# A one-core encoder layer on Trainium2: sum transfers at two points of a quad instead of three, stores and tiles moved, another product order in w_down, and dummy matmuls at the start

## The chip, the cores and the metric

The kernel runs on one core of a Trainium2 chip. The metric is the device time of one execution in microseconds, the median of the runs shown. Of the core's engines, PE (TensorE) multiplies matrices, DVE (VectorE), ACT (ScalarE) and POOL (GpSimd) work elementwise, and SP (SyncE) issues transfers. Transfers are issued by the sequencers of SP, POOL and, rarely, ACT, each with a queue of its own.

## The reference, cut to what matters

```python
D_MODEL = 2048; SEQ = 512; D_FF = 5632          # one layer, batch 1, float32
mod = (silu(c) @ w_ada + b_ada)[:, None, :]
sh_m, sc_m, gt_m, sh_f, sc_f, gt_f = split(mod, 6)
h = x * (1 + sc_m) + sh_m
y = mixer_sublayer(h, ...)     # linear recurrence (8 heads) and sparse attention (16 heads),
                               # merged by sigmoid gates, projected by w_out
x = layer_norm(ALPHA * x + (1 + gt_m) * y, ln1_g, ln1_b)
h = x * (1 + sc_f) + sh_f
y = (silu(h @ w_gate) * (h @ w_up)) @ w_down
x = layer_norm(ALPHA * x + (1 + gt_f) * y, ln2_g, ln2_b)
```

The change touches the start (silu(c)), the attention loop, and above all the last three lines: the two products with w_gate and w_up, the product with w_down, and the last norm.

## The kernel before

Weights stay in float32 in DRAM. Each weight tile is fetched into a tile `raw` (128x1024, 512 KB), and split into two parts of fewer bits: ACT writes the high part `whi` (L272), DVE the rest `wlo` = raw − whi (L273). The left operand is split in the same way, and a product is three matmuls (high·high at L237, two mixed ones at L238 and L239). PE keeps its sums in PSUM.

The products with w_gate, w_up and w_down are done over 2x2 blocks of both operands with seven products of blocks instead of eight (`SEVEN`, L127: p1, q7, r6, p2, q5, q4, p3). Four of them need sums of weight blocks: S1 = 21+22, S2 = S1+11, S3 = 21+11 and S4 = S2+12, where 11 to 22 name the blocks.

**Gate and up.** A group, called a quad, is the seven products of one 2x2 quad of w_gate or w_up: `("gu", n)`, even n for gate, odd n for up; 44 of them, 40 (n from 4) in one loop of steps, each step one product of 24 matmuls. For these 40, a table (`fetch`, L1253) gives the step at which SP issues the fetches of the four blocks, counted back from the quad's first step: 11 at 7 steps, 21 at 6, 22 and 12 at 5 (L1268). DVE adds the sums S1 to S4 (L1271 to L1285) in `raw` tiles, of which there are five. For the w_down groups (`("dn", n, cc)`, 22 of them) and the first quads the sums are made ahead by transfers from DRAM to DRAM, 512 KB each, on the POOL queue (`add_up`, L993): a first one that copies a block, then ones that accumulate. There are 208 such jobs in one list. `more(n)` takes the next n from it: four per attention head, some in the projections after it, and the rest in the gate/up loop, one at each of q7, r6 and p2 of a quad, each behind a small POOL copy (`pace`, L1602) that waits for that product's result. A job list of `sum_jobs` is ordered by kind: all copies into S3, all into S1, then accumulates into S3 and S1, then copies into S2, and so on.

After an up quad, `give` (L1423) makes from the activations the left operands of w_down (DVE, tiles `r`) and stores them in seven transfers of 128 KB (names d_p, d_q, d_r) on SP's queue (L1436). All transfers of SP run through one sequencer in program order: an issue that waits for its data holds the ones behind it.

**Down.** The loop goes on with 154 units (product, n, cc) of 12 matmuls of 512 columns: products in the order of `SEVEN`, and for each the 11 pairs n and 2 column halves cc. Beside it, generators called side lanes are advanced after every half unit. `base_side` (L1504) has POOL load two rows of norm weights (`ln`, L1510) and scale them (L1511), load a stored tile `base` of the residual (L1515), and DVE (L1519) and POOL (L1522, L1523) norm it. `end_side` takes finished output tiles: `join` multiplies by the gate row `gtf` (L1531), adds base (L1532) and takes norm statistics (L1533); `norm` (L1535) applies the last layer norm, half of it on ACT and POOL, half on DVE (L1544, L1545), and stores. The last four units keep their split weights (`KEEP`, tiles `wkeep`): p3 for rows t+2, run piece by piece so that the end can follow each piece.

The row `gtf` (1 MB, L1065) is loaded on the POOL queue before the gate/up loop, in the one buffer with the tag "row" of the constant pool. At the start PE spreads the vector c over the partitions (L192), ACT takes its silu, and the first product waits for weights and h.

Of the kernel before, what the change touches and what calls it, by code (L numbers as in the profile page):

```python
# [31 lines left out]
P = 128  # L32
D = 2048
T = 512
# [90 lines left out]


SEVEN = ("p1", "q7", "r6", "p2", "q5", "q4", "p3")  # L127
NP2 = NF // 2


# [9 lines left out]
def layer_kernel(ctx, tc, ws, wa, wada, xt, x, cin, bada, lbl, ghg, gcq, gckv, ln1c, lnrow, ident, lvm, dist, out):  # L140
# [51 lines left out]
        mmul(spread[i], one_t[:1], cond[:1, i * T:(i + 1) * T], start=True, stop=True)  # L192
    for i in range(4):
        nc.scalar.activation(cond[:, i * T:(i + 1) * T], spread[i], AF.Silu)
    del spread


# [802 lines left out]
            add_up(*jobs.pop(0))  # L1000

    for h in range(SAH):
        more(4)
        at_query(h)
        if h >= 2:
            at_transpose(h - 2)
        if h == SAH - 1:
            del cqn_hi, cqn_lo
            ylo = [big(f"yalo{i}") for i in range(2)]
            for n in range(HGH):  # L1010
                yar.append(heap("yarel"))
# [231 lines left out]
    for n in range(NPRE, 2 * NP2):  # L1243
        steps += [Unit(("gu", n), i) for i in SEVEN]
    nsteps = len(steps)
    steps += [Unit(("dn", n, cc), i) for i in SEVEN for n in range(NP2 // 2) for cc in range(2)]
    raws = {}

    fetch, adds = {}, {}
    for n in range(NPRE, 2 * NP2):  # L1250
        s = NPRE * 7 + (n - NPRE) * 7
        for ahead, what in ((7, "11"), (6, "21"), (5, "22"), (5, "12")):
            fetch.setdefault(s - ahead, []).append((("gu", n), what))  # L1253
        for ahead, what in ((3, "S3"), (3, "S1"), (2, "S2"), (-2, "S4")):
            adds.setdefault(s - ahead, []).append((("gu", n), what))
# [123 lines left out]
    def gu_use(u):  # L1379
        n, i = u.group[1], u.i  # L1380
        p, up = n // 2, n % 2
        ps = acc[n, CHAIN[i]][:, :H]
        t = tmp.setdefault(n, {})
        if i == "p1":
            t["e"] = heap("e")
            nc.scalar.activation(t["e"][:, :H], ps, AF.Copy)  # L1386
        elif i == "q7":
            t["yv"] = heap("yv")
            nc.scalar.activation(t["yv"][:, :H], ps, AF.Copy)  # L1389
            acc_copy[:] = [t["yv"][:, :1]]  # L1390
        elif i == "r6":
            nc.scalar.activation(t["yv"][:, H:], ps, AF.Copy)
            acc_copy[:] = [t["yv"][:, H:H + 1]]
        elif i == "p2":
            e = t.pop("e")[:, :H]
            acc_copy[:] = [e[:, :1]]
            if up:
                nc.vector.tensor_add(e, e, ps)
                nc.vector.tensor_mul(act[p][:, :H], act[p][:, :H], e)
            else:  # L1400
                a = act[p] = heap("act")
                nc.vector.tensor_add(a[:, :H], e, ps)
                nc.scalar.activation(a[:, :H], a[:, :H], AF.Silu)
        elif i == "q5":
            vq = heap("vq")[:, :H]
            t["c"] = heap("c") if up else heap("act")
            nc.scalar.activation(vq, ps, AF.Copy)  # L1407
            nc.vector.tensor_sub(t["c"][:, H:], t["yv"][:, :H], vq)
        elif i == "q4":
            c = t.pop("c")  # L1410
            nc.vector.tensor_sub(c[:, :H], ps, t.pop("yv")[:, H:])
            if up:
                nc.vector.tensor_mul(act[p + NP2], act[p + NP2], c)
            else:
                act[p + NP2] = c
                nc.scalar.activation(c, c, AF.Silu)
        elif up:
            a, b = act.pop(p), act.pop(p + NP2)
            nc.vector.tensor_mul(a[:, H:], a[:, H:], ps)
            give(p, a, b)  # L1420
        else:
            nc.scalar.activation(act[p][:, H:], ps, AF.Silu)
        if i in DONE:  # L1423
            del acc[n, CHAIN[i]]

    def give(p, a, b):

        r, q = heap("r"), heap("r")
        sub = nc.vector.tensor_sub
        sub(r[:, :H], a[:, :H], a[:, H:])  # L1430
        sub(r[:, H:], a[:, H:], b[:, H:])
        sub(q[:, :H], r[:, H:], a[:, :H])
# [40 lines left out]
    def dn_use(u):  # L1473
# [5 lines left out]
        for t in range(2):  # L1479
# [4 lines left out]
            elif i == "q7":  # L1484
                nc.scalar.activation(part["Y"][:, j], ps, AF.Copy)
            elif i == "r6":
                nc.vector.tensor_sub(part["V"][:, j], part["Y"][:, j], ps)
            elif i == "p2":
                nc.vector.tensor_add(part["E"][:, j], part["E"][:, j], ps)
                ends.append((t, cc, part["E"][:, j]))  # L1490
            elif i == "q5":
                nc.vector.tensor_sub(part["Y"][:, j], part["Y"][:, j], ps)
                ends.append((t + 2, cc + 2, part["Y"][:, j]))
            elif i == "q4":
                nc.vector.tensor_add(part["V"][:, j], part["V"][:, j], ps)
                ends.append((t, cc + 2, part["V"][:, j]))
            if CHAIN[i] != "V":
                del acc[CHAIN[i], cc, t]
            del ps

# [25 lines left out]
    st2 = [cp.tile([P, 24], FT, name=f"sf{t}", tag=f"st{t}") for t in range(NT)]  # L1526
    rows2 = []

    def join(t, c, y, ps=None):

        nc.vector.tensor_mul(y, y if ps is None else ps, gtf[:, c * T:c * T + T])  # L1531
        nc.vector.tensor_add(y, y, base.pop((t, c)))  # L1532
        nc.vector.bn_stats(st2[t][:, c * 6:c * 6 + 6], y)  # L1533
        done[t, c] = y

    def norm(t, c, mv, on_pool):

        z, g, b = done.pop((t, c)), rows2[0][c], rows2[1][c]
        if on_pool:
# [2 lines left out]
            nc.gpsimd.tensor_add(z, z, b)  # L1542
        else:
            nc.vector.scalar_tensor_tensor(z, z, mv[:, 0:1], g, op0=OP.subtract, op1=OP.mult)  # L1544
            nc.vector.scalar_tensor_tensor(z, z, mv[:, 3:4], b, op0=OP.mult, op1=OP.add)  # L1545
        (nc.scalar if on_pool and t == NT - 1 else nc.sync).dma_start(out[t * P:t * P + P, c * T:c * T + T], z)

    def end_side():

# [6 lines left out]
        for n in range(12):  # L1556
            while not ends:
                yield
            join(*ends.pop(0))
            yield  # L1560
            yield
        for t in range(2):
            mv = ln_scale(st2[t], "mv2")
            for c in range(4):
                norm(t, c, mv, c % 2 == 0)
                yield
                yield
# [7 lines left out]
    for step in range(len(steps)):  # L1575
# [19 lines left out]
        if step == 3 * NPRE + 2:  # L1595
            for t in range(NT):
                side.drain(t)
            assert not hraw
            gtf = gate_row(1, "gtf")
        if u.group[0] == "gu" and u.group[1] >= NPRE and u.i in ("q7", "r6", "p2"):  # L1600

            nc.gpsimd.tensor_copy(pace, acc_copy[0])  # L1602
            more(1)
        if step == nsteps - 1:
# [6 lines left out]
            for i in "EYV":  # L1611
                part[i] = big(i, FT)
            side.add(0, base_side())
            side.add(1, end_side())
    res = big("res", FT)
    for t in range(2):
        for cc in range(2):
            for u in steps[len(steps) - KEEP:]:
                if u.group[2] == cc:
                    dn_mm(u, t)  # L1620
            join(t + 2, cc, res[:, 2 * cc + t], acc["V", cc, t])
        if t == 0:
            side.drain(0)
            side.drain(1)
        mv = ln_scale(st2[t + 2], "mv2")
        for c in (2, 3, 0, 1):
            norm(t + 2, c, mv, c < 2 if t == 0 else c == 0)


# [101 lines left out]
```

## Time and profile before

| | |
|---|---|
| median of 3 runs | 2841.31 us (2840.8 to 2846.91) |
| the profiled execution, own time | 2842.75 us |
| its span in the trace | 2841.0 us |
| PE busy | 2757.5 us, 97% |
| DVE, ACT, POOL busy | 72%, 41%, 22% |
| chain that ended last | PE 78%, DVE 8%, DMA 7% |
| start, until PE is steadily busy | 0 to 44 us |
| mixer, attention, projections | 44 to about 1450 us |
| gate/up loop, first to last copy of a quad's first product (L1386) | 1560.28 to 2371.37 us |
| down units | about 2387 to 2811 us |
| last units and end | to 2841.0 us |

Read the busy shares as averages: PE is busy nearly all the time, so what matters is where it waits, and whom it waits for. In rows of a timeline the bracket gives the idle time of that engine before the row, and what ended it. Rows with SPq are transfer issues on SP's sequencer; their second column is how long the issue took the sequencer.

### The profile page before, as it was taken

The page shows a single profiled execution, that of the slowest core. Times are in us where ns is not written, and L with a number is a line of the kernel's source. Part 1 is how long each engine was busy: PE and PEld are TensorE (multiplying, and loading weights), DVE is VectorE, ACT ScalarE, POOL GpSimd, SP SyncE. Part 2 cuts the span into 40 slices and gives each one's busy share as a digit, 9 for nine tenths or more (in the row PEclk, how much of TensorE's full clock was granted, in tenths as well). Part 3 has the DMA queues.
Part 4 walks back from the last instruction along what each step waited for, and adds up shares of the span by engine and source line. Part 5 has one row for each costly group of instructions (what it writes and reads, how often), then busy time and mean ns, then how long its engine had stood idle before and what let it go on. Part 6 is the DMA issues. An engine that isn't in the chain of part 4 may idle for free.

```text
span 2841.0 us, 41802 instructions
## 1 busy us (share of the span) xinstructions
PE 2757.5 (97%) x16034; PEld 2425.5 (85%) x16034; DVE 2042.3 (72%) x2878; ACT 1161.8 (41%) x1725; POOL 636.3 (22%) x807
## 2 busy tenths in 40 slices
PE   7999999999999999999999999999989999999996
PEld 5778888888888888888889999899989999887885
DVE  7877787778852777446667776777767777766777
ACT  4334434333222555222255443444434444554443
POOL 0011133342010764312110112111111001443003
PEclk9999999999999999999999999999999999999998
DMA  9866445556974875977945657666676346888764
GB/s 378 311 209 216 158 155 175 178 181 202 325 264 148 237 240 174 336 203 213 272 145 178 233 199 193 189 193 217 181 187 168 127 145 205 277 275 276 236 222 167
DMA packets 194058, 609.86 MB, mean 215 GB/s; under 512 B 23201, under 2 KB 43217, under 8 KB 190785
## 3 DMA queue, kind: packets, MB, share of 16 engines
q1 hardware_dynamic: 149186, 450.63, 46.2%
q0 software_dynamic: 44384, 156.24, 20.5%
q8 instruction: 126, 2.06, 0.3%
q14 instruction: 74, 0.61, 0.1%
q10 hardware_dynamic: 288, 0.31, 0.0%
HBM read 564.09 MB, written 149.70 MB: 251 GB/s over the span
## 4 chain that ended last, share of the span: by engine, by line
PE 78%; DVE 8%; DMA 7%; issue 3%; ACT 2%; POOL 1%; SPq 0%; DVEq 0%; ACTq 0%; POOLq 0%
PE gb L229 6%; PE y L229 6%; PE ga L229 6%; DMA raw<-in_ws 5%; PE V L237 4%; PE V L239 4%; PE V L238 4%; PE qb L229 3%; PE pb L229 3%; PE g L229 3%; PE v L229 3%; DVE wlo L273 3%; PE pa L229 3%; PE early L229 2%; PE s L229 2%
## 5 line engine op out<-in xcount | busy, mean ns | idle before, releaser
L273 DVE TENSOR_TENSOR wlo<-raw,whi 128x1024 fp32r<-128x1024 f32 x458 | 568.1, 1252 | 265.5 <-ACT whi L272 263.7
L272 ACT ACTIVATE whi<-raw 128x1024 fp32r<-128x1024 f32 x458 | 482.4, 1058 | 479.3 <-DVE raw L1275 93.6
L359 DVE TENSOR_TENSOR wlo<-raw,whi 128x1024 fp32r<-128x1024 f32 (+1 forms) x228 | 284.5, 1251 | 110.0 <-ACT whi L347 109.5
L347 ACT ACTIVATE whi<-raw 128x1024 fp32r<-128x1024 f32 (+1 forms) x228 | 233.7, 1038 | 206.9 <-DVE raw L1082 72.3
L237 PE MATMUL V<-mhi,whi 128*128 128x256 f32 x1056 | 301.8, 286 | 14.8 <-ACT vq L1407 14.8
L239 PE MATMUL V<-mhi,wlo 128*128 128x256 f32 x1056 | 300.8, 285 | 0.0
L238 PE MATMUL V<-mlo,whi 128*128 128x256 f32 x1056 | 300.7, 285 | 0.0
L237 PEld LDWEIGHTS V<-mhi,whi 128*128 128x128 f32 x1056 | 204.4, 194 | 16.3 <-ACT vq L1407 16.1
L1602 POOL COPY pace<-yv 128x1 f32<-128x1 f32 x80 | 55.9, 699 | 691.5 <-ACT yv L1389 627.8
L239 PE MATMUL Y<-R,wlo 128*128 128x256 f32 x704 | 198.5, 282 | 11.2 <-DVE wlo L273 11.2
L239 PEld LDWEIGHTS V<-mhi,wlo 128*128 128x128 f32 x1056 | 204.4, 194 | 0.0
L238 PEld LDWEIGHTS V<-mlo,whi 128*128 128x128 f32 x1056 | 204.3, 193 | 0.0
L237 PE MATMUL Y<-R,whi 128*128 128x256 f32 x704 | 198.3, 282 | 1.0 <-ACT whi L272 1.0
L238 PE MATMUL Y<-R,whi 128*128 128x256 f32 x704 | 197.8, 281 | 0.0
L239 PEld LDWEIGHTS Y<-R,wlo 128*128 128x128 f32 x704 | 135.0, 192 | 12.6 <-DVE wlo L273 12.6
L238 PE MATMUL dnV<-wlo,fhi 128*128 128x512 f32 x336 | 132.7, 395 | 8.4 <-DVE wlo L273 8.3
L237 PEld LDWEIGHTS Y<-R,whi 128*128 128x128 f32 x704 | 135.1, 192 | 1.2 <-ACT whi L272 1.2
L238 PEld LDWEIGHTS Y<-R,whi 128*128 128x128 f32 x704 | 135.3, 192 | 0.0
L239 PE MATMUL dnV<-whi,flo 128*128 128x512 f32 x336 | 132.7, 395 | 0.0
L237 PE MATMUL dnV<-whi,fhi 128*128 128x512 f32 x336 | 132.4, 394 | 0.0
L993 POOL DMA_DIRECT2D sum_dn<-in_ws x132 | 96.6, 846 | 38.7 <-DMA sum_dn<-in_ws 31.2
L237 PE MATMUL V<-R,whi 128*128 128x256 f32 x352 | 98.2, 279 | 4.4 <-ACT e L1386 4.4
(450 smaller groups left out, 7562.4 us busy)
## 6 DMA issues: line engine op xcount, KB each, us to landing
raw<-in_ws SPq DMA_DIRECT2D x454, 512.0 KB, 5.0
sum_dn<-in_ws POOLq DMA_DIRECT2D x132, 512.0 KB, 9.4
raw<-in_wada SPq DMA_DIRECT2D x128, 512.0 KB, 5.0
raw<-sum_dn SPq DMA_DIRECT2D x88, 512.0 KB, 4.4
rawb<-in_wada SPq DMA_DIRECT2D x22, 1024.0 KB, 12.0
sum_dn<-sum_dn POOLq DMA_DIRECT2D x44, 512.0 KB, 6.5
sum_gu<-in_ws POOLq DMA_DIRECT2D x24, 512.0 KB, 8.7
raws<-in_wada SPq DMA_DIRECT2D x40, 256.0 KB, 6.9
```

The source lines that it names most:

```text
L229: mmul(*a, **k)
L237: f(ps, ahi, bhi, start=first, stop=False, **k)
L238: f(ps, ahi, blo, start=False, stop=False, **k)
L239: f(ps, alo, bhi, start=False, stop=last, **k)
L272: nc.scalar.activation(hi, src, AF.Copy)
L273: engine.tensor_sub(lo, src, hi.bitcast(FT))
L347: nc.scalar.activation(hi, src, AF.Copy)
L359: nc.vector.tensor_sub(lo, src, hi.bitcast(FT))
L993: nc.gpsimd.dma_start(d_sum[g, dst], block(g, src), **({"accum_op": OP.add} if add else {}))
L1602: nc.gpsimd.tensor_copy(pace, acc_copy[0])
```

## The change

The sum transfers in the gate/up loop are issued at q7 and q5 of a quad, not at q7, r6 and p2; every second attention head takes five in place of four. The fetches of a quad move to 8, 8, 6 and 4 steps ahead. Block 12 and the sum S3 no longer take `raw` tiles: they share a tile `wrow` in the buffer with the tag "row", so that `gtf` is loaded after the loop instead of before it. The stores of `give` move from SP's to POOL's queue. The order of products in w_down is p1, q7, r6, q5, p3, p2, q4. Rows t+2 are then finished first, through a part "R", with joins and norms spread over more yields; norms beside the products run on DVE alone. Six units are kept for the end; their piece is q4's. After the silu of c, 28 matmuls of 128x128 are issued whose results nobody reads.

```diff
+DOWN_SEVEN = ("p1", "q7", "r6", "q5", "p3", "p2", "q4")
...
+    for n in range(28):
+        mmul(spread[n % 4][:, :P], one_t, one_t, start=True, stop=True)
     del spread
...
     for h in range(SAH):
-        more(4)
+        more(4 + h % 2)
...
-    steps += [Unit(("dn", n, cc), i) for i in SEVEN for n in range(NP2 // 2) for cc in range(2)]
+    steps += [Unit(("dn", n, cc), i) for i in DOWN_SEVEN for n in range(NP2 // 2) for cc in range(2)]
...
-        for ahead, what in ((7, "11"), (6, "21"), (5, "22"), (5, "12")):
+        for ahead, what in ((8, "11"), (8, "21"), (6, "22"), (4, "12")):
...
-            r = raws[group, what] = new_raw()
+            if what == "12":
+
+                row = cp.tile([P, D], FT, name="wrow", tag="row")
+                raws[group, "S3"], r = row[:, :1024], row[:, 1024:]
+            else:
+                r = new_raw()
+            raws[group, what] = r
...
-                r = raws[g, "S3"] = new_raw()
-                add(r, raws[g, "21"], raws[g, "11"])
+                add(raws[g, "S3"], raws[g, "21"], raws[g, "11"])
...
-            nc.sync.dma_start(d_r[i, p // 2][:, p % 2], v)
+            nc.gpsimd.dma_start(d_r[i, p // 2][:, p % 2], v)
...
+        for t in (2, 3):
             mv = ln_scale(st2[t], "mv2")
             for c in range(4):
-                norm(t, c, mv, c % 2 == 0)
+                for _ in norm(t, c, mv):
+                    yield
...
-    KEEP = 4
+    KEEP = 6
...
-            gtf = gate_row(1, "gtf")
-        if u.group[0] == "gu" and u.group[1] >= NPRE and u.i in ("q7", "r6", "p2"):
+        if u.group[0] == "gu" and u.group[1] >= NPRE and u.i in ("q7", "q5"):
...
+            gtf = gate_row(1, "gtf")
             side.add(0, base_side())
             side.add(1, end_side())
-    res = big("res", FT)
+    side.drain(0)
+    side.drain(1)
...
+            ps, y, v = acc.pop(("Y", cc, t)), heap("y"), part["V"][:, 2 * cc + t]
+            nc.vector.tensor_mul(y, ps, gtf[:, (cc + 2) * T:(cc + 3) * T])
+            nc.vector.tensor_add(y, y, v)
+            nc.vector.bn_stats(st2[t][:, (cc + 2) * 6:(cc + 3) * 6], y)
...
+        for c in (0, 1, 2, 3):
+            for _ in norm(t, c, mv, c == 0, nc.scalar if c == 0 else nc.sync):
+                pass
```

On SP's queue in the middle of the gate/up loop, the kernel before issues the seven stores of a pair of quads (d_p, d_q, d_r; act and r are the activations) between the fetches of two quads each:

```order
L1436 DMA d_p_6_10665<-act 128x256
L1436 DMA d_q_6_10676<-r 128x256
L1436 DMA d_r_6_10687<-r 128x256
L1436 DMA d_p_6_10698<-act 128x256
L1436 DMA d_q_6_10709<-r 128x256
L1436 DMA d_q_6_10720<-r 128x256
L1436 DMA d_p_6_10731<-act 128x256
L1268 DMA raw<-in_ws 128x1024 x8
L1436 DMA d_p_7_10666<-act 128x256
```

and the changed kernel, in the same stretch:

```order
L1278 DMA raw<-in_ws 128x1024 x3
L1278 DMA wrow<-in_ws 128x1024
L1278 DMA raw<-in_ws 128x1024 x3
L1278 DMA wrow<-in_ws 128x1024
L1278 DMA raw<-in_ws 128x1024 x3
```

The stores have left SP's queue, and the fourth fetch of each quad goes to wrow.

On POOL's queue where the gate/up loop ends and the down units begin, the kernel before has the last pace copies and then the rows of `base_side`:

```order
L1602 COPY pace<-yv 128x1 x2
L1602 COPY pace<-e 128x1
L1510 DMA ln_22638<-in_lnrow 128x512
L1511 TENSOR_SCALAR ln_22638<-ln_22638 128x512
L1510 DMA ln_22639<-in_lnrow 128x512
L1511 TENSOR_SCALAR ln_22639<-ln_22639 128x512
L1515 DMA base<-d_z 128x512
```

and the changed kernel:

```order
L997 DMA sum_dn_1_4_7313<-in_ws 128x1024
L1444 DMA d_p_10_10705<-act 128x256
L1444 DMA d_q_10_10716<-r 128x256
L1444 DMA d_r_10_10727<-r 128x256
L1444 DMA d_p_10_10738<-act 128x256
L1444 DMA d_q_10_10749<-r 128x256
L1444 DMA d_q_10_10760<-r 128x256
L1444 DMA d_p_10_10771<-act 128x256
L1069 DMA gtf<-d_row 128x2048
L1518 DMA ln_22587<-in_lnrow 128x512
L1519 TENSOR_SCALAR ln_22587<-ln_22587 128x512
L1518 DMA ln_22588<-in_lnrow 128x512
```

Seven stores, a last sum and the load of gtf now stand ahead of the first `ln`.

On DVE near the end of the down units, the kernel before does a join's three operations in a row between two splits of weights (V is an output part):

```order
L273 TENSOR_TENSOR wlo<-raw,whi 128x1024
L1531 TENSOR_TENSOR V<-V,gtf 128x512
L1532 TENSOR_TENSOR V<-V,base 128x512
L1533 BN_STATS sf_12018<-V 128x6
L1495 TENSOR_TENSOR V<-V,dnY 128x512 x2
L273 TENSOR_TENSOR wlo<-raw,whi 128x1024
L273 TENSOR_TENSOR flo<-raws,fhi 128x512
L1531 TENSOR_TENSOR V<-V,gtf 128x512
L1532 TENSOR_TENSOR V<-V,base 128x512
L1533 BN_STATS sf_12019<-V 128x6
```

and the changed kernel, where V only takes gtf and base there:

```order
L277 TENSOR_TENSOR wlo<-raw,whi 128x1024
L1577 TENSOR_TENSOR V<-V,gtf 128x512
L1579 TENSOR_TENSOR V<-V,base 128x512
L277 TENSOR_TENSOR wlo<-raw,whi 128x1024
L277 TENSOR_TENSOR flo<-raws,fhi 128x512
L1577 TENSOR_TENSOR V<-V,gtf 128x512
L1579 TENSOR_TENSOR V<-V,base 128x512
```

At most two operations of this side work now stand between two splits, and the two subtractions that read dnY have gone from this place.

## Rows read from the trace of the kernel before

**Rows 1.** Timeline of ACT, line L1386: start us, us, operation [idle before<-releaser].
```profile
1560.28 0.36 ACT L1386 ACTIVATE e<-V 128x256 f32<-128x256 f32 x1
1599.64 0.37 ACT L1386 ACTIVATE e<-V 128x256 f32<-128x256 f32 x1
...
1717.78 0.36 ACT L1386 ACTIVATE e<-V 128x256 f32<-128x256 f32 x1
...
1743.69 0.37 ACT L1386 ACTIVATE e<-V 128x256 f32<-128x256 f32 x1
...
2351.34 0.36 ACT L1386 ACTIVATE e<-V 128x256 f32<-128x256 f32 x1
```

**Rows 2.** Timeline of SP's issues, 1707 to 1726 us.
```profile
1707.65 0.33 SPq L1436 DMA_DIRECT2D d_p<-act  x1
1719.34 0.33 SPq L1436 DMA_DIRECT2D d_q<-r  x1
...
1722.59 2.92 SPq L1268 DMA_DIRECT2D raw<-in_ws  x4
```

**Rows 3.** Timeline of POOL, 1720 to 1727 us.
```profile
1725.41 1.10 POOL L993 DMA_DIRECT2D sum_dn<-in_ws  x1
```

**Rows 4.** Chain of waits, 1700 to 1780 us: start us, us, what.
```profile
1723.67 13.81 DMA raw<-in_ws
```

**Rows 5.** Transfers issued, 1560 to 1700, then 1710 to 1900: KB, median us to landing.
```profile
raw<-in_ws SPq DMA_DIRECT2D x29, 512.0 KB, 6.1
...
raw<-in_ws SPq DMA_DIRECT2D x32, 512.0 KB, 9.3
```

**Rows 6.** Timelines of SP and POOL, 2380 to 2400 us.
```profile
2388.86 0.33 SPq L1436 DMA_DIRECT2D d_q<-r  x1
...
2385.51 0.58 POOL L1510 DMA_DIRECT2D ln<-in_lnrow  x1 [4.38 <-DVE flo L273]
...
2398.93 0.59 POOL L1515 DMA_DIRECT2D base<-d_z  x1
```

**Rows 7.** Timelines of DVE and PE, 2404 to 2412 us.
```profile
2405.41 0.55 DVE L1519 TENSOR_SCALAR base<-base,mv 128x512 f32<-128x512 f32 x1 [4.79 <-DMA base<-d_z]
...
2411.07 0.51 PE L238 MATMUL dnV<-wlo,fhi 128*128 128x512 f32 x1 [0.90 <-DVE wlo L273]
```

**Rows 8.** Transfers issued, whole span, and line L993 in 1560 to 1700 (issue ns min/median/max).
```profile
gtf<-d_row POOLq DMA_DIRECT2D x1, 1024.0 KB, 7.3
...
L993 POOL DMA_DIRECT2D sum_dn<-sum_dn x21: 515/515/536, 1563.8 to 1686.0; - x21
```

**Rows 9.** Waits, 2391 to 2812 us: us in total, times, longest us.
```profile
PE dnV L238 <- DVE wlo L273: 8.3, 5, 3.2
```

**Rows 10.** Timeline of PE, 2779 to 2782 us.
```profile
2780.38 0.50 PE L238 MATMUL dnV<-wlo,fhi 128*128 128x512 f32 x1 [3.17 <-DVE wlo L273]
...
2781.30 0.63 PE L238 MATMUL dnV<-wlo,fhi 128*128 128x512 f32 x1
```

**Rows 11.** Timelines of DVE, 2817 to 2841 us, and of PE, 2821 to 2824 us.
```profile
2817.26 0.69 DVE L1531 TENSOR_TENSOR res<-dnV,gtf 128x512 f32<-128x512 f32 x1 [0.60 <-PE dnV L239]
...
2836.28 0.75 DVE L1545 SCALAR_TENSOR_TENSOR res<-res,mv,l 128x512 f32<-128x512 f32 x1
...
2822.32 0.40 PE L239 MATMUL dnV<-wkeep,flo 128*128 128x512 f32 x1
```

**Rows 12.** POOL's waits 915 to 1125 us, its timeline 965 to 975, chain 915 to 1000.
```profile
POOL sum_gu L993 <- DMA sum_gu<-in_ws: 9.2, 4, 3.0
...
969.47 0.73 POOL L1016 TENSOR_TENSOR first<-qb 128x256 f32<-128x256 f32 x1
...
978.00 3.56 PE s L229 x22
```

**Rows 13.** Timeline of PE, 0 to 24 us.
```profile
2.63 7.16 PE L192 MATMUL cond<-cond,one_t 1*128 1x512 f32 x8 [2.63 <-DMA cond<-in_cin]
...
21.49 0.79 PE L229 MATMUL a<-hTlo,whi 128*128 128x512 f32 x1 [2.24 <-DVE hTlo L467]
```

More of the change, by code (lines that the diff above doesn't have):

```diff
@@ L1392, in gu_use @@
             nc.scalar.activation(t["yv"][:, H:], ps, AF.Copy)
-            acc_copy[:] = [t["yv"][:, H:H + 1]]
         elif i == "p2":
             e = t.pop("e")[:, :H]
-            acc_copy[:] = [e[:, :1]]
             if up:
@@ L1407, in gu_use @@
             nc.scalar.activation(vq, ps, AF.Copy)
+            acc_copy[:] = [vq[:, :1]]
             nc.vector.tensor_sub(t["c"][:, H:], t["yv"][:, :H], vq)
@@ L1487, in dn_use @@
                 nc.vector.tensor_sub(part["V"][:, j], part["Y"][:, j], ps)
-            elif i == "p2":
-                nc.vector.tensor_add(part["E"][:, j], part["E"][:, j], ps)
-                ends.append((t, cc, part["E"][:, j]))
             elif i == "q5":
@@ L1493, in dn_use @@
                 ends.append((t + 2, cc + 2, part["Y"][:, j]))
[L1494 to L1497, printed above, removed]
+            elif i == "p3":
+                nc.scalar.activation(part["R"][:, j], ps, AF.Copy)
+                ends.append((t + 2, cc, part["R"][:, j]))
+            else:
+                nc.vector.tensor_add(part["E"][:, j], part["E"][:, j], ps)
+                ends.append((t, cc, part["E"][:, j]))
+            if i in ("q7", "p3", "p2"):
                 del acc[CHAIN[i], cc, t]
@@ L1527, in layer_kernel, with join, norm @@
     rows2 = []
-    def join(t, c, y, ps=None):
-        nc.vector.tensor_mul(y, y if ps is None else ps, gtf[:, c * T:c * T + T])
+    def join(t, c, y):
+        nc.vector.tensor_mul(y, y, gtf[:, c * T:c * T + T])
+        yield
         nc.vector.tensor_add(y, y, base.pop((t, c)))
+        yield
         nc.vector.bn_stats(st2[t][:, c * 6:c * 6 + 6], y)
         done[t, c] = y
-    def norm(t, c, mv, on_pool):
+    def norm(t, c, mv, on_pool=False, q=None):
         z, g, b = done.pop((t, c)), rows2[0][c], rows2[1][c]
@@ L1544, in norm @@
             nc.vector.scalar_tensor_tensor(z, z, mv[:, 0:1], g, op0=OP.subtract, op1=OP.mult)
+            yield
             nc.vector.scalar_tensor_tensor(z, z, mv[:, 3:4], b, op0=OP.mult, op1=OP.add)
-        (nc.scalar if on_pool and t == NT - 1 else nc.sync).dma_start(out[t * P:t * P + P, c * T:c * T + T], z)
+        (q or nc.sync).dma_start(out[t * P:t * P + P, c * T:c * T + T], z)
     def end_side():
@@ L1555, in end_side @@
                 nc.gpsimd.dma_start(rows2[n][c], lnrow[2 + n][:, c * T:c * T + T].to_broadcast([P, T]))
-        for n in range(12):
+        for n in range(8):
             while not ends:
                 yield
-            join(*ends.pop(0))
-            yield
+            for _ in join(*ends.pop(0)):
+                yield
             yield
         for t in range(2):
+            for cc in range(2):
+                v = part["V"][:, 2 * cc + t]
+                nc.vector.tensor_mul(v, v, gtf[:, (cc + 2) * T:(cc + 3) * T])
+                yield
+                nc.vector.tensor_add(v, v, base.pop((t, cc + 2)))
+                yield
+        for t in (2, 3):
             mv = ln_scale(st2[t], "mv2")
             for c in range(4):
-                norm(t, c, mv, c % 2 == 0)
+                for _ in norm(t, c, mv):
+                    yield
                 yield
+        del part["Y"], part["R"]
+        for n in range(4):
+            while not ends:
                 yield
-    KEEP = 4
+            for _ in join(*ends.pop(0)):
+                yield
+            yield
+    KEEP = 6
     for u in steps[len(steps) - KEEP:]:
@@ L1610, in layer_kernel @@
             small = lambda name, dt=FT: yp.tile([P, T], dt, name=name, tag="y")
-            for i in "EYV":
+            for i in "EYVR":
                 part[i] = big(i, FT)
+            gtf = gate_row(1, "gtf")
             side.add(0, base_side())
             side.add(1, end_side())
-    res = big("res", FT)
+    side.drain(0)
+    side.drain(1)
+    assert not jobs and not ends
     for t in range(2):
@@ L1620, in layer_kernel @@
                     dn_mm(u, t)
[L1621 to L1627, printed above, removed]
+            ps, y, v = acc.pop(("Y", cc, t)), heap("y"), part["V"][:, 2 * cc + t]
+            nc.vector.tensor_mul(y, ps, gtf[:, (cc + 2) * T:(cc + 3) * T])
+            nc.vector.tensor_add(y, y, v)
+            nc.vector.bn_stats(st2[t][:, (cc + 2) * 6:(cc + 3) * 6], y)
+            done[t, cc + 2] = y
+        mv = ln_scale(st2[t], "mv2")
+        for c in (0, 1, 2, 3):
+            for _ in norm(t, c, mv, c == 0, nc.scalar if c == 0 else nc.sync):
+                pass
 def token_order():
```

## The prediction

> **What bounds the kernel now.** I read the page's busy shares first: PE 97%, so a gain must come out of PE's own waits, or out of the start and the end. Then the timeline of one ACT line that recurs once a quad, which shows where the gate/up loop runs late; there the timelines of SP and POOL and the chain of waits for the reason; then the waits in the down units; then the last DVE and PE rows.
>
> The copy of a quad's first product (L1386) is a clock for the loop [rows 1]. From 1560.28 to 1599.64 are two quads, 39.36 us, while nothing is late. From 1560.28 to 2351.34 are 38 quads, 791.06 us; at 39.36 a pair they would take 19 x 39.36 = 747.84. So 43.2 us are lost in this loop. A late quad is that from 1717.78 to 1743.69: 25.91 us, 6.2 more than 39.36 / 2. In the stretch 1560 to 1700 no time goes, and the sums there are copies; the time goes while accumulating sums run.
>
> Why it is late: SP starts the first store of a pair at 1707.65, and the next at 1719.34, since it waits for DVE's `r` [rows 2]. For 11.4 us it can issue no fetch. Once the stores are out, it issues four fetches back to back at 1722.59, 2.92 us of sequencer time. At the same moment POOL issues its sums, the last at 1725.41 [rows 3]. The raw tile that comes of it takes 13.81 us in the chain [rows 4], where the median landing is 6.1 us in the quiet stretch and 9.3 in the late one [rows 5]. DVE's sums of blocks, the split and PE wait for that tile.
>
> **The change part by part.** The sum is made against the profiled execution's 2842.75 us, 1.4 above the median of 2841.31; the same 1.4 is taken off at the end.
>
> *Gate/up loop.* The seven stores leave SP, so its 11.4 us hold is gone. Fetches 11, 21 and 22 are issued a step or two earlier, block 12 a step later. A step is 19.68 / 7 = 2.81 us. Block 22 now has about three steps, 8.4 us, to the sum that reads it, block 12 about four, 11.2 us. Both cover the quiet landing of 6.1, and block 12 also the 9.3 [rows 5]; beyond that PE has three steps of split weights ahead of it. Two sums a quad, at products two steps or more apart, in place of three, thin out the bursts; the 44 accumulates in the loop stay 44, over 22 quads in place of about 15. Ends: all 43.2 back, or nothing (if the accumulates themselves, not the bunching, slow the fetches). I take −41, near the full end, because quads lose no time at all in the quiet stretch with the same SP burst: it needs burst and accumulates together, and both are made smaller. The issue of seven stores on POOL costs it 7 x 0.52 = 3.6 us a pair by the row of its sum issues [rows 8], of 39.36, on an engine busy 22%.
>
> The Trainium skill, "SBUF — State Buffer", section "SBUF: two separate sides", says that descriptors for transfers from POOL's queue can't be written while DVE runs an operation in a mode that holds the port that the two share. If that held here, seven stores issued beside a busy DVE would be stretched, say to 1.2 us each as an estimate, and the next part would be 7 x 0.7 = 5 us dearer. The trace does not agree: 21 sum issues took 515 to 536 ns with DVE 72% busy [rows 8].
>
> *From the loop to the down units.* Here the move costs. Before, POOL issues the first `ln` load at 2385.51 and the first base load at 2398.93, 13.4 us later, after two loads and two scalings [rows 6]. DVE waits 4.79 us for that tile at 2405.41, and PE, which needs the splits behind it, waits 0.90 at 2411.07 [rows 7]: the cover is just used up. After, POOL's queue has six stores that wait for data from 2388.86 on [rows 6], and `gtf`, ahead of that `ln`. Six stores and gtf at 0.52 end at 2388.9 + 7 x 0.52 = 2392.5, so the chain starts 7.0 us later; `gtf`, 1 MB, took 7.3 to land [rows 8] and shares the queue with the `ln` tiles. The base operation stands at the same place in DVE's order, so that what comes later PE pays. The shift is 7.0 if the rest runs as before, 7.0 + 7.3 = 14.3 if the load waits for all of gtf. It is less if the two loads go faster than before, when stores and fetches ran beside them. I take 8.5, nearest to the 7.0, plus 1.7 for about eight matmuls at the low clock after a PE wait (0.63 us each against 0.40 [rows 10, 11]): +10. Ends: 0 and +18.
>
> *Down units.* Five PE waits for `wlo`, 8.3 us [rows 9]. One is the 0.90 above. The longest is 3.17 at 2780.38 [rows 10], where a join's three operations in a row stand ahead of the splits and norms run beside them; after it matmuls show 0.63, the 1.2 GHz level in place of 2.4, some 1.7 us more. With one or two operations between splits, and no operation on POOL beside DVE's, I take −4 of these 4.9. Ends: nothing, or all but the 0.90 with the clock, −9.
>
> *End.* From the second piece's join at 2817.26 to 2841.0 are 23.7 us. PE's last matmul ends at 2822.7, and 18.3 us follow it [rows 11]. After, one more norm pair on DVE (2 x 0.75) makes 25.3. But two pieces of 18 matmuls still stand behind that join (36 x 0.229 = 8.2 us) in place of two of 12 (5.5). So 25.3 − 8.2 = 17.1 follow PE's end: −1.2. Ends −3 and +3 (two more norms at 0.75 each, or two joins fewer in the way).
>
> *Attention.* Eight more transfers, four by head 7. POOL waits 9.2 us in four waits for earlier sums [rows 12]. The nearest reader is `first`, written at 969.47, and PE comes to its use at 978.00: 8.5 − 0.73 = 7.8 us of cover. Each transfer adds about 0.5 of issue and 2.3 of wait (9.2 / 4), 2.8; four are 11.2 by head 7, so at worst 3.4 are uncovered there, and twice that if it recurs: 0 to +6. POOL's bias work has gaps before it, so I take +1.
>
> *Start.* The spread of c took 7.16 us for eight passes of 512 columns [rows 13], 0.22 per 128. 28 matmuls in two passes are 56 x 0.22 = 12.5 us from about 10, to about 23. The second product waits till 21.49 anyway [rows 13], so the delay is at most 1.5; a clock that is up earlier can give some 2 back (12 matmuls x 0.2). Between them I take 0; ends −2 and +3.
>
> Sum: −41 + 10 − 4 − 1.2 + 1 + 0 = −35.2. 2842.75 − 35.2 = 2807.5, less 1.4 is 2806.
>
> **The rivals.**
> *No junction cost.* The loads at the junction run faster without stores beside them, or DVE gets a reserve from an unstalled loop. For: the two `ln` loads shared the engines with stores and fetches. Against: the wait of 0.90 is there already. With all 43.2 back: 2841.3 − 43.2 − 4 − 1.2 + 1 = 2794.
>
> *The burst moves to POOL.* The stores wait on POOL for `r` as they did on SP, with the sum of the next quad behind them, so that sums and stores come out together with the fetches of 11 and 21, and half of the gain stays away: −20.5 in place of −41: 2826.5. For: the 11.4 us hold is data, not SP. Against: the fetches are no longer in that queue.
>
> *The accumulates are the price.* The 13.81 us come from accumulating transfers sharing the DMA engines with fetches, whoever issues them and when; the same 44 then cost the same 43, and the junction comes on top: 2841.3 + 10 − 4 − 1.2 + 1 = 2847, slower. It decides as soon as the loop gives back less than 5.8 (10 − 4.2). For: only stretches with accumulates lose time. Against: the late quads all have the four fetches issued in one burst just after the hold [rows 2]. The Trainium skill, "DMA: Bandwidth & Descriptors", section "Issuing engines are not separate DMA queues", speaks for this rival: it says that issuing from another engine saves only sequencer time, since all transfers share the same engines. By it the move of the stores alone would give the loop nothing but SP's hold; the trace shows that this hold is 11.4 us of sequencer time before the burst [rows 2].
>
> *A wash.* The junction at its dear end and a third of the gain cancel to within 0.2%.
>
> **How the numbers follow.** The forecast's case 0.47 (2798 to 2815), no junction cost 0.20, half of the loop 0.18, accumulates 0.10, wash 0.05. 0.2% is 5.7 us, about what a measurement here can tell from no change. Faster 0.47 + 0.20 + 0.18 = 0.85, same 0.05, slower 0.10. The range reaches from the second case with 4 us for a better end or down part, 2790, to the third with 5.5 for a dearer junction, 2832. It leaves out 0.15.
>
> **What would show it.** Right: the copies of L1386's counterpart 39.4 us a pair throughout, so that 38 quads take about 750; no SP issue with a hold over a few us; raw landings near 6; PE waiting some 8 us near 2375, behind a DVE wait for base of over 10; no PE wait of 3 us late in the down units; about 17 us between PE's last matmul and the end. Wrong: quads of 25 us while accumulates run, raw tiles of over 12 us in the chain, or PE waits for `whi` or `wlo` in the attention heads.

## The result, and the profile after

The changed kernel takes 2803.07 us (median of 4 runs, 2800.0 to 2807.84) against 2844.11 for the kernel before (4 runs): 41.0 us less, ratio 0.9855 with a 95% interval of 0.983 to 0.9881. The forecast was 2806 and 35.3 less than the median then shown. The profiled execution has a span of 2798.0 us against 2841.0. These 43.0 us divide as follows:

| stretch | before | after | difference | forecast |
|---|---|---|---|---|
| start to the first copy in the loop (first product of quad n = 4) | 1560.28 | 1561.24 | +1.0 | +1 |
| 38 quads of the gate/up loop | 791.06 | 747.89 | −43.2 | −41 |
| from there to the first down matmul | 36.07 | 36.09 | 0.0 | 0 |
| down units, to PE's last matmul | 435.31 | 436.48 | +1.2 | +10 − 4 |
| after PE's last matmul | 18.28 | 16.30 | −2.0 | −1.2 |

The timeline of ACT's copy of each quad's first product, which answers to [rows 1] (L1395 is L1386 of before):

```profile
1561.24 0.36 ACT L1395 ACTIVATE e<-V 128x256 f32<-128x256 f32 x1
1600.60 0.36 ACT L1395 ACTIVATE e<-V 128x256 f32<-128x256 f32 x1
...
1718.74 0.36 ACT L1395 ACTIVATE e<-V 128x256 f32<-128x256 f32 x1
...
1738.77 0.37 ACT L1395 ACTIVATE e<-V 128x256 f32<-128x256 f32 x1
...
2309.13 0.36 ACT L1395 ACTIVATE e<-V 128x256 f32<-128x256 f32 x1
```

A pair takes 39.36 us as in the quiet stretch before, and so do all 19, within 0.06. The quad that took 25.9 us takes 20.0, the longer of the two alternating quads that make 39.36.

What the 43.2 us of the kernel before were made of, its waits of PE from 1560 to 2352 us show (us in total, times, longest):

```profile
PE V L237 <- ACT vq L1407: 14.8, 6, 6.6
PE Y L239 <- DVE wlo L273: 10.4, 6, 2.3
PE V L237 <- ACT e L1386: 4.4, 4, 1.4
```

These are 29.6 us; the changed loop has no such wait. The other 13.6 are matmuls that follow each other more slowly: the granted clock was 0.5 in five stretches of the loop before, 23.9 us in all, and 1.00 in the whole of the changed loop. So nearly a third of the gain is not waiting but the pace of matmuls around the waits.

SP's timeline in the stretch of [rows 2], then POOL's, shows where the wait for `r` went:

```profile
1705.36 0.33 SPq L1278 DMA_DIRECT2D wrow<-in_ws  x1
1705.79 18.02 SPq L1278 DMA_DIRECT2D raw<-in_ws  x3
```
```profile
1711.62 0.88 POOL L1444 DMA_DIRECT2D d_p<-act  x1
1720.57 0.57 POOL L1444 DMA_DIRECT2D d_q<-r  x1 [8.07 <-DVE r L1439]
...
1724.57 0.88 POOL L997 DMA_DIRECT2D sum_dn<-in_ws  x1
```

POOL now waits 8.07 us for DVE, and a sum comes out behind the stores, but no fetch stands there. SP's 18 us are three fetches, the last of which waits for a free tile until 1723.48. SP's waits for a free tile from 1600 to 2300 us are long, up to 15.4 us, and cost the loop nothing:

```profile
SPq L1278 <- DVE wlo L277: 508.2, 36, 15.4
```

The transfers of 1710 to 1900 us, answering to the second of [rows 5]:

```profile
raw<-in_ws SPq DMA_DIRECT2D x28, 512.0 KB, 7.1
...
wrow<-in_ws SPq DMA_DIRECT2D x9, 512.0 KB, 7.7
```

At the junction, POOL's timeline, then DVE's and PE's, answer to [rows 6, 7]:

```profile
2346.94 0.57 POOL L1444 DMA_DIRECT2D d_q<-r  x1 [4.78 <-DVE r L1439]
...
2350.69 0.54 POOL L1518 DMA_DIRECT2D ln<-in_lnrow  x1
2361.50 1.50 POOL L1519 TENSOR_SCALAR ln<-ln 128x512 f32<-128x512 f32 x1 [10.27 <-DMA ln<-in_lnrow]
...
2368.13 0.58 POOL L1523 DMA_DIRECT2D base<-d_z  x1
```
```profile
2371.11 0.55 DVE L1527 TENSOR_SCALAR base<-base,mv 128x512 f32<-128x512 f32 x1 [15.13 <-DMA base<-d_z]
```
```profile
2372.84 0.80 PE L242 MATMUL dnV<-wlo,fhi 128*128 128x512 f32 x1 [8.01 <-DVE wlo L277]
2373.43 0.63 PE L243 MATMUL dnV<-whi,flo 128*128 128x512 f32 x1
...
2376.37 0.40 PE L241 MATMUL dnV<-whi,fhi 128*128 128x512 f32 x1
```

POOL waits 10.27 us for the first `ln`, DVE 15.13 for the base tile, PE 8.01; eight matmuls follow at the lower clock level (granted 0.5 from 2369.5 to 2376.3), as forecast. PE's waits for splits from 2340 us on ([rows 9]):

```profile
PE dnV L242 <- DVE wlo L277: 10.4, 3, 8.0
```

Beside the 8.0 only two short ones are left; the 3.17 late in the down units [rows 10] is gone. The end, DVE then PE, answers to [rows 11]:

```profile
2773.49 0.69 DVE L1650 TENSOR_TENSOR y<-dnY,gtf 128x512 f32<-128x512 f32 x1 [1.97 <-PE dnY L243]
...
2793.67 0.75 DVE L1556 SCALAR_TENSOR_TENSOR y<-y,mv,l 128x512 f32<-128x512 f32 x1
```
```profile
2781.30 0.40 PE L243 MATMUL dnY<-wkeep,flo 128*128 128x512 f32 x1
```

### The profile page after: what moved, and what is told of

It is laid out like the page before. It is cut to its first block, busy times and chain, and to the rows that moved or that the text cites. A ratio compares the mean times of both kernels' runs of the same rounds, so it can differ in the third digit from the quotient of the medians.

```text
span 2798.0 us, 41846 instructions
## 1 busy us (share of the span) xinstructions
PE 2750.3 (98%) x16090; PEld 2421.6 (87%) x16090; DVE 2040.0 (73%) x2892; ACT 1158.3 (41%) x1724; POOL 675.6 (24%) x911
## 4 chain that ended last, share of the span: by engine, by line
PE 90%; DVE 4%; DMA 3%; issue 2%; ACT 1%; POOL 1%; SPq 0%; DVEq 0%; POOLq 0%; ACTq 0%
PE gb L233 6%; PE y L233 6%; PE ga L233 6%; PE V L243 6%; PE V L241 6%; PE V L242 6%; PE qb L233 3%; PE pb L233 3%; PE g L233 3%; PE v L233 3%; PE Y L241 3%; PE Y L243 3%; PE Y L242 3%; PE pa L233 3%; PE early L233 2%; PE dnV L242 2%
## 5 line engine op out<-in xcount | busy, mean ns | idle before, releaser
L277 DVE TENSOR_TENSOR wlo<-raw,whi 128x1024 fp32r<-128x1024 f32 x376 | 468.4, 1253 | 235.4 <-ACT whi L276 235.3
L276 ACT ACTIVATE whi<-raw 128x1024 fp32r<-128x1024 f32 x376 | 397.5, 1058 | 345.2 <-PE dnV L243 132.8
L242 PE MATMUL dnV<-wlo,fhi 128*128 128x512 f32 x352 | 139.1, 395 | 10.4 <-DVE wlo L277 10.4
L243 PE MATMUL dnV<-whi,flo 128*128 128x512 f32 x352 | 138.7, 394 | 0.0
L276 ACT ACTIVATE whi<-wrow 128x1024 fp32r<-128x1024 f32 x80 | 84.4, 1055 | 84.7 <-DVE wrow L1284 84.7
L233 PE MATMUL ga<-hThi,whi 128*128 128x512 f32 x256 | 102.0, 398 | 0.0
```

What stands on the lines that cost most here:

```text
L233: mmul(*a, **k)
L242: f(ps, ahi, blo, start=False, stop=False, **k)
L243: f(ps, alo, bhi, start=False, stop=last, **k)
L276: nc.scalar.activation(hi, src, AF.Copy)
L277: engine.tensor_sub(lo, src, hi.bitcast(FT))
```

## The experiments

The theory from the prediction: the loop is late where two things meet, SP's hold behind the stores with a burst of fetches after it, and accumulating sums. Its rivals: three sums a quad alone, the fetch table and the buffers alone, the accumulates alone. The measure is the time of 38 quads, from each run's own trace. It is far sharper than a run's total: ten of these runs give 747.9 to within 0.05.

| run | 38 quads | down units | after PE's end | time |
|---|---|---|---|---|
| before (profiled) | 791.1 | 435.3 | 18.3 | 2842.75 |
| changed (profiled) | 747.9 | 436.5 | 16.3 | 2800.09 |
| a_stores_sp | 747.9 | 436.2 | 16.7 | 2798.46 |
| a_three_sums | 747.9 | 437.8 | 16.3 | 2802.83 |
| a_old_fetch | 747.9 | 438.0 | 16.3 | 2803.3 |
| b_copies | 748.3 | 434.6 | 19.8 | 2801.17 |
| b_stores_pool | 748.2 | 444.4 | 17.9 | 2809.96 |
| b_two_sums | 760.0 | 441.4 | 18.3 | 2822.2 |
| b_new_fetch | 747.9 | 438.6 | 18.3 | 2801.37 |
| a_keep4 | 747.9 | 436.5 | 19.0 | 2804.08 |
| a_again | 747.9 | 440.5 | 16.3 | 2805.99 (median) |
| a_gtf_late | 747.9 | 435.4 | 16.3 | 2802.83 |
| a_sp_gtf_late | 747.9 | 430.9 | 16.7 | 2795.89 (median) |
| a_no_dummies | 747.9 | 439.1 | 16.3 | 2804.62 |

**One edit of the changed kernel undone.** a_stores_sp:

```diff
-            nc.gpsimd.dma_start(d_r[i, p // 2][:, p % 2], v)
+            nc.sync.dma_start(d_r[i, p // 2][:, p % 2], v)
```

> The changed kernel with the seven stores of a pair back on SP's queue. Measure: 38 quads of the gate/up loop by the copy of each quad's first product (before 791.1 us, changed 747.9). Theory of the prediction (SP held for 11 us by the stores, then fetches in a burst while accumulates run): most of the loss comes back, 770 to 791, with SP holds of about 11 us and quads of 23 to 26 us in the accumulating stretch alone. Rival 'sums': three sums a quad are the cause, so it stays at 748 to 755. Rival 'fetch table and buffers': earlier fetches and the tile outside the five raw buffers are the cause, so it stays at 748 to 755 too. The junction to the down units should lose less than the changed kernel's 8.0 us, as POOL no longer has stores ahead of the norm rows: 0 to 4.

747.9: the theory's number fell. SP's hold is there, as its timeline shows, and costs nothing:

```profile
1704.33 2.31 SPq L1278 DMA_DIRECT2D raw<-in_ws  x2
1707.10 0.33 SPq L1444 DMA_DIRECT2D d_p<-act  x1
1718.84 0.33 SPq L1444 DMA_DIRECT2D d_q<-r  x1
```

From 1707.10 to 1718.84 SP issues no fetch. But the two fetches just before the hold are blocks 11 and 21 of a quad to come: the new table puts them ahead of the stores in SP's order, where the old one had them behind. The junction's PE wait was 4.85, more than the 0 to 4 expected.

a_three_sums:

```diff
-        if u.group[0] == "gu" and u.group[1] >= NPRE and u.i in ("q7", "q5"):
+        if u.group[0] == "gu" and u.group[1] >= NPRE and u.i in ("q7", "r6", "p2"):
...
+            acc_copy[:] = [t["yv"][:, H:H + 1]]
...
+            acc_copy[:] = [e[:, :1]]
...
-            acc_copy[:] = [vq[:, :1]]
```

> The changed kernel with one sum transfer at each of q7, r6 and p2 of a quad, as before. 38 quads: theory of the prediction: stores no longer hold SP, so little comes back, 748 to 758. Rival 'sums': 775 to 791, with late quads while accumulates run, until the list is empty, some 15 quads of them. Rival 'fetch table and buffers': 748 to 752.

747.9: three sums a quad are not a sufficient cause.

a_old_fetch, which also gives block 12 and S3 raw tiles again:

```diff
-        for ahead, what in ((8, "11"), (8, "21"), (6, "22"), (4, "12")):
+        for ahead, what in ((7, "11"), (6, "21"), (5, "22"), (5, "12")):
```

> The changed kernel with the fetches at 7, 6, 5 and 5 steps ahead again and with block 12 and S3 in the five raw tiles; gtf is still loaded after the loop. 38 quads: theory of the prediction: 748 to 760, since stores and sums are eased. Rival 'sums': 748 to 752. Rival 'fetch table and buffers': 775 to 791, with long waits of SP for a raw tile.

747.9: nor are the fetch table and buffers. Each of the three edits can be missed as long as the other two stand.

**One thing taken from the kernel before.** b_copies:

```diff
-        nc.gpsimd.dma_start(d_sum[g, dst], block(g, src), **({"accum_op": OP.add} if add else {}))
+        nc.gpsimd.dma_start(d_sum[g, dst], block(g, src), **({"accum_op": OP.add} if add and g[0] == "gu" else {}))
```

> The kernel before, with every accumulating transfer for the w_down sums made a plain copy of the same 512 KB (the sums of w_down are then not formed; the work of all engines is otherwise the same). 38 quads: if accumulates are a necessary part, no quad is late and it takes 748 to 753. If the hold of SP alone does it, the loss stays at 780 to 791; the stretch 1560 to 1700, where copies run and nothing is late, speaks against that.

748.3: the accumulates are necessary. With the same bytes written, three transfers a quad, SP's hold and the old table, 0.4 of the 43 us is left. How an accumulate differs from a copy shows in POOL's queue from 1710 to 1850 us (packets, MB, share of the 16 DMA engines' time), in the kernel before, then in b_copies:

```profile
q0 software_dynamic: 2812, 10.21, 38.6%
q0 software_dynamic: 3051, 11.13, 22.4%
```

Per MB the packets of the accumulating transfers took 1.9 times as long, on the engines that the fetches use too. Their issue took longer too, 0.81 us in the median against 0.52; which of the two makes the fetches late is not shown.

b_stores_pool is the reverse of the first edit, on the kernel before:

```diff
-            nc.sync.dma_start(d_r[i, p // 2][:, p % 2], v)
+            nc.gpsimd.dma_start(d_r[i, p // 2][:, p % 2], v)
```

> The kernel before with only the seven stores of a pair moved to POOL's queue. 38 quads (before 791.1, changed 747.9). Theory of the prediction, that SP's hold and the fetch burst behind it make the loss: 748 to 755 by this edit alone. Rival 'any one relief is enough' (undoing each edit alone left the loop at 747.9): 748 to 755 for this and for each of the next two. Rival 'fetch table and buffers first': 775 to 791 here, since the fetches of blocks 22 and 12 still come at 5 steps and the raw tiles stay five.

748.2: moving the stores alone gives the whole loop back, as the theory said; "fetch table and buffers first" is out. The fetches of 1710 to 1900 us land in 5.2 us (median) in place of 9.3, although the same accumulates run. But its down units take 444.4, 9.1 more than before: PE waits 4.07 at the junction, where POOL's stores stand ahead of the norm rows (3.2 more), 2.1 more at other places, and 3.9 are slower matmuls.

b_two_sums:

```diff
-        if u.group[0] == "gu" and u.group[1] >= NPRE and u.i in ("q7", "r6", "p2"):
+        if u.group[0] == "gu" and u.group[1] >= NPRE and u.i in ("q7", "q5"):
...
-        more(4)
+        more(4 + h % 2)
```

> The kernel before with two sums a quad (at q7 and q5) and five transfers at every second attention head. 38 quads: theory of the prediction: the hold is there, bursts are thinner: 760 to 780. Rival 'any one relief is enough': 748 to 755. Rival 'fetch table and buffers first': 775 to 791.

760.0: 31 of 43 us come back, at the theory's edge; "any one relief is enough" misses here. Its late quads are shorter, as ACT's copies in the stretch of the 25.9 us quad show:

```profile
1721.93 0.36 ACT L1386 ACTIVATE e<-V 128x256 f32<-128x256 f32 x1
1743.47 0.37 ACT L1386 ACTIVATE e<-V 128x256 f32<-128x256 f32 x1
```

21.5 us in place of 25.9.

b_new_fetch is the reverse of a_old_fetch on the kernel before, with the load of gtf after the loop:

```diff
-        for ahead, what in ((7, "11"), (6, "21"), (5, "22"), (5, "12")):
+        for ahead, what in ((8, "11"), (8, "21"), (6, "22"), (4, "12")):
...
+                row = cp.tile([P, D], FT, name="wrow", tag="row")
+                raws[group, "S3"], r = row[:, :1024], row[:, 1024:]
...
+            gtf = gate_row(1, "gtf")
             side.add(0, base_side())
```

> The kernel before with the new fetch table and the tile outside the raw buffers for block 12 and S3 (so gtf is loaded after the loop, ahead of the norm rows on POOL). SP still holds 11 us at the stores. 38 quads: theory of the prediction: some of the loss stays, 755 to 775. Rivals 'any one relief is enough' and 'fetch table and buffers first': 748 to 752. The junction should show the price of gtf alone: a PE wait of 4 to 6 us in place of 0.9, as the run with the stores on SP had 4.8.

747.9, where the theory wanted 755 to 775. Its transfers land no sooner than those of before in 1710 to 1900 us:

```profile
raw<-in_ws SPq DMA_DIRECT2D x28, 512.0 KB, 9.7
...
wrow<-in_ws SPq DMA_DIRECT2D x10, 512.0 KB, 8.2
```

So long landings as such are not the loss: with 9.7 us as with the 9.3 of before, PE never waits in this loop. Here too blocks 11 and 21 go out ahead of the hold. But the edit also gives the fetches a sixth tile (`wrow`), and no run has the new table with five tiles: which of the two does it is not shown. Of the three edits made alone, this is the only one that is within the range of the whole change (2801.37, one run). The price of gtf was overestimated: PE waits 2.15 at the junction, not 4 to 6.

**The end.** a_keep4:

```diff
-    KEEP = 6
+    KEEP = 4
```

> The changed kernel with four units kept for the end in place of six. By the prediction's working, two pieces of 12 matmuls (5.5 us) stand behind the second join in place of two of 18 (8.2), so 2.7 us more follow PE's last matmul: 19.0 in place of 16.3. Rival: DVE is not what orders the end and it stays at 16.3 within 0.5.

19.0, exactly the working's number: DVE's chain from the second join orders the end, and what counts is how much of PE's work still stands behind that join.

**The junction.** a_again is the changed kernel, timed again beside the next.

> The changed kernel again, timed on the same chip as the next. Expected some 41 us under the kernel before (ratio 0.9855), with the loop at 747.9 and the PE wait of 8.0 at the junction to the down units.

Median 2805.99 (ratio 0.9863, 0.9844 to 0.9882), 36.7 under the kernel before where some 41 were expected; the loop takes 747.9, the PE wait is 8.47.

a_sp_gtf_late, with the edit of a_stores_sp and:

```diff
-            gtf = gate_row(1, "gtf")
             side.add(0, base_side())
...
+        if step == nsteps + 22:
+            gtf = gate_row(1, "gtf")
```

> The changed kernel with the stores on SP's queue and the load of gtf 22 units later, behind the first norm rows. Theory of the prediction on the junction (stores and gtf ahead of the norm rows on POOL's queue make the base tile late, and PE pays): the PE wait there falls from 8.0 to about 1, the low clock behind it goes, and the down units take 428 to 431 in place of 436.5, so 6 to 8 us under the changed kernel, ratio 0.982 to 0.984 to the kernel before. Rival 'given back later': base tiles run at a fixed pace, so what is not waited for here is waited for at a later base tile: the down units stay at 434 to 437.

Median 2795.89 (2794.61 to 2798.67; ratio 0.983, 0.9811 to 0.9848), 10.1 under the changed kernel on the same chip, whose runs span 2803.18 to 2806.54. The down units take 430.9, inside the 428 to 431; that is 5.6 and 9.6 under the two profiled executions of the changed kernel. PE's wait at the junction is 6.2 and 6.7 shorter, so of the 10.1, more than the 6 to 8 expected, some 6 are the junction's; much of the rest is the slower pace of one execution described at the end. This is the fastest version. "Given back later" is out for it, but not in general: a_stores_sp waits 3.2 us less at the junction than the changed kernel, and its down units are only 0.3 shorter, with a new wait of 1.61 at 2425.0 and 1.4 more of slow matmuls. PE's wait at the first base tile:

```profile
2370.72 0.51 PE L242 MATMUL dnV<-wlo,fhi 128*128 128x512 f32 x1 [1.78 <-DVE wlo L277]
```

a_gtf_late has this diff alone, the stores still on POOL.

> The changed kernel with gtf 22 units later, its stores still on POOL. It parts the two pieces of the junction: gtf alone (stores on SP, gtf ahead) left a PE wait of 4.8 and both 8.0. If the pieces add up, the stores alone leave 3 to 4; if the last one to land decides, 0.9 to 2.

Neither number: the wait is 5.73. With neither in the way 1.78, gtf alone 4.85, stores alone 5.73, both 8.01: 3.1 and 3.9 over 1.78, together 6.2. They add up nearly, above a floor that I had set at zero.

The floor is a third piece, the last sum, which two sums a quad put 4.45 us ahead of the first down matmul. All runs together show how the pieces act. The base operation on DVE is given in us after the first down matmul, and PE's wait is that for the split behind it:

| run | ahead of the norm rows on POOL | base operation | PE's wait |
|---|---|---|---|
| before | nothing | 18.00 | below 0.15 |
| a_sp_gtf_late | sum | 19.66 | 1.78 |
| b_new_fetch | gtf | 20.03 | 2.15 |
| b_two_sums | sum | 21.74 | 3.85 |
| b_stores_pool | stores | 21.95 | 4.07 |
| a_stores_sp | sum, gtf | 22.73 | 4.85 |
| a_gtf_late | sum, stores | 23.61 | 5.73 |
| a_three_sums | gtf, stores | 25.15 | 7.27 |
| changed | sum, stores, gtf | 25.89 | 8.01 |

In each row but the first the wait is the base operation's time less 17.88, to 0.01: what delays the base tile, PE pays in full. In the kernel before, the matmul behind it waits too little to be listed; the 0.90 of [rows 7] is at the next split:

```profile
2407.14 0.50 PE L238 MATMUL dnV<-wlo,fhi 128*128 128x512 f32 x1
```

Why the same sum leaves 1.78 in one run and 3.85 in another is open.

**The start.** a_no_dummies:

```diff
-    for n in range(28):
-        mmul(spread[n % 4][:, :P], one_t, one_t, start=True, stop=True)
```

> The changed kernel without the 28 dummy matmuls. Prediction's term: 0, between -2 and +3, so the copy of the fourth quad's first product (1561.24) moves by less than 3 us. In the first 45 us: with the dummies PE's first products run at the 2.4 GHz level from the start, without them at the 1.2 GHz level for some 8 us; rival 'the clock counts': 2 to 4 us later at 45 us without them; rival 'the weights' stream decides': within 0.5 at 45 us.

The first product runs 0.48 us after the dummies, 0.79 without (PE's timeline of the changed kernel, then of this one):

```profile
9.87 8.60 PE L198 MATMUL cond<-one_t 128*128 128x128 f32 x56
18.23 0.48 PE L233 MATMUL a<-hThi,whi 128*128 128x512 f32 x1
20.63 0.50 PE L233 MATMUL a<-hTlo,whi 128*128 128x512 f32 x1 [1.92 <-DVE hTlo L471]
...
21.27 0.63 PE L233 MATMUL a<-hThi,whi 128*128 128x512 f32 x1
```
```profile
19.54 0.79 PE L231 MATMUL a<-hThi,whi 128*128 128x512 f32 x1 [9.79 <-ACT hThi L466]
```

But 1.92 us of waiting later the changed kernel's matmuls are at 0.63 too (granted 0.5 from 21.1 to 24.5). The copy of n = 4 comes at 1563.42 without the dummies, 1561.24 and 1563.79 in two executions of the changed kernel. At 45 us nothing is gained that shows: the next stage (tile `early`) starts at 49.1 without the dummies, at 47.5 and 49.0 with them. So the dummies' worth is below the spread, and the two rivals are not told apart.

## Why the prediction was right

**The loop, −41, was −43.2.** That all of it can be had was right. Both halves of the cause are shown: without accumulates (b_copies) or without the hold (b_stores_pool) the loop is whole. What I had not seen is that a third condition must hold as well, the old fetch table with five tiles. With the new one the hold remains and nothing is late (a_stores_sp, b_new_fetch); whether the earlier fetches or the sixth tile does it is not shown. The change thus carries two remedies that suffice each by itself, and a third, the two sums, that gives 31. The late quad of the prediction was 5.9 us late, not 6.2, since the two quads of a pair differ. Two signs of being right did not come: SP still shows holds, up to 15.4 us, with no loss, and fetches land in 7.1 us, not near 6.

**From the loop to the down units, +10, was about +8.5.** The wait grew from 0.90 to 8.01, 7.1, and eight matmuls at the lower level cost some 1.7 (0.43 apart in place of 0.229, by the timeline above), 1.4 more than the slow ones behind the wait before. The shift was sized from issues and the landing of gtf at 8.5; the base operation came 7.9 later (25.89 in place of 18.00). That this is so near is partly luck: the base issue came 22.9 us after the first down matmul (2368.13 − 2345.22) in place of 11.5 (2398.93 − 2387.41), 11.4 later, but the base tile then landed in 3.0 us in place of 6.5. The last sum was not in the prediction's list of what stands ahead. a_sp_gtf_late shows the mechanism: without stores and gtf ahead, most of it goes.

**Down units, −4, was the term most mis-sized: about −7.3.** With +8.5 at the junction and +1.2 in all, the rest gave −7.3. Four waits of 7.4 us in all became two of 2.4: −5.0; matmuls further apart than 0.229 us, outside the junction, cost 3.6 before and 1.2 after: −2.4. The two late waits, 3.2 and 1.8 to 2.0 us, are in all five runs of the kernel before and its variants and in none of the changed kernel's. That the order of products, the spread joins or the norms on DVE alone removed them is argued from the order of DVE's operations: no run undoes one of these.

**The end, −1.2, was −2.0.** The chain from the second join took 24.5 us (2773.49 to 2798.0), not 25.3. The 8.2 us of PE behind it were right, and a_keep4 confirms the working.

**Start, 0, can't be told from the spread.** The 28 dummies took 8.60 us and ended at 18.47, not 12.5 and 23, so they did not delay the second product.

**Attention, +1, was 0.** The first uv matmul to the first pb matmul takes 219.8 us in both kernels (910.8 to 1130.6, 911.9 to 1131.7). POOL's wait for earlier sums did grow, from 9.2 [rows 12] to 12.9, under cover. The +1.0 at 1560 is there by 442 us, and is part of the spread: that copy lay between 1558.8 and 1565.4 over the runs.

**The rivals.** "No junction cost" is out (8.01). "The burst moves to POOL": the hold did move there, 8.07 us, and cost the loop nothing, since the fetches no longer stood behind it. "The accumulates are the price" is out: the same 44 run, and the loop is whole. They are a necessary condition, not a price. The Trainium skill says that another issuing engine saves only the sequencer's time to initiate a transfer ("DMA: Bandwidth & Descriptors", "Issuing engines are not separate DMA queues"). In these traces initiating is the small part, 0.33 us for a store on SP [rows 2]. What b_stores_pool took off SP was above all the wait for data, 11.4 us a pair, and that was enough for 43 us. The Trainium skill's port rule ("SBUF — State Buffer", "SBUF: two separate sides") did not show: the 154 stores on POOL took 0.54 to 0.89 us each, not the 1.2 that was given as an estimate. Whether any operation of DVE here holds that port is not shown.

## What to carry to other kernels

A stall that needs several conditions at once goes when any of them goes, and shrinks when one is only eased. Undoing one edit of a good change then proves nothing about that edit: do each one alone on the kernel before as well. When transfers move to another queue, look at the place where that queue next has urgent work: here moving 154 stores that cost the loop nothing, one row and the last sum cost PE 7 us at a single point, and keeping stores and row out of the way was worth some 6. At the end of a kernel, count what PE still has to do behind the second-to-last piece, since the other engine's chain runs beside it.

## What the runs showed that I had not expected

The same kernel's down units took 436.5 and 440.5 us in two executions. The pitch of matmuls differs between about 2400 and 2540 us: 0.2289 us on average in the one, 0.2333 in the other, at a granted clock of 1.00 in both by the stretches of 10 us from 2385 on. Rows of PE from the execution with 440.5, then from the other:

```profile
2469.60 0.40 PE L243 MATMUL dnY<-whi,flo 128*128 128x512 f32 x1
...
2470.77 0.40 PE L242 MATMUL dnY<-wlo,fhi 128*128 128x512 f32 x1
```
```profile
2469.77 0.39 PE L241 MATMUL dnY<-whi,fhi 128*128 128x512 f32 x1
...
2470.92 0.39 PE L243 MATMUL dnY<-whi,flo 128*128 128x512 f32 x1
```

Five starts take 1.17 us in the first and 1.15 in the second. The stretch with the longer pitch came after the junction's wait, where the clock fell and rose, and ended about the next waits, of 1.27 and 0.90 us, at 2536 to 2541; over some 155 us it costs 3. Another 1 is the clock at 0.5 for 10.2 us at the junction in place of 6.8. The kernel before has the longer pitch too, between its low clock behind the wait of 3.17 [rows 10] and its next wait at 2795.19: these two rows are 35 starts apart, 0.2331 us each:

```profile
2784.84 0.40 PE L238 MATMUL dnV<-wlo,fhi 128*128 128x512 f32 x1
...
2793.00 0.39 PE L237 MATMUL dnV<-whi,fhi 128*128 128x512 f32 x1
```

What sets it is open. It is one reason why totals of one kernel differ by several us while its loop agrees to 0.05.
